# GpSimd's residual row scalings of the second layer: from the retention core into the rotary and gate items

## The chip, the cores and the metric

The kernel runs on one core of a Trainium2 chip, in one launch. The metric is device time in microseconds (us) from the start to the end of that launch. The kernel before took 2866.8 us, the median of three runs (2865.53 to 2873.29).

A core has five engines with queues of their own: TensorE (matmuls, PE in the profile, with its weight loads as PEld), VectorE (DVE), ScalarE (ACT), GpSimd (POOL) and SyncE (SP), which here only issues DMA transfers. ScalarE and GpSimd can issue transfers too. All transfers share 16 DMA engines.

## The reference

The model is a trunk of two layers on one sequence of 1024 rows of 1024 features, in float32. Layer 0 mixes with a gated delta network, layer 1 with retention; each layer ends with a gated feed-forward network. What matters here is the second layer's first half:

```python
for i in range(DEPTH):
    mod = (e @ ada_w[i] + ada_b[i])[:, None, :]
    sh1, sc1, g1, sh2, sc2, g2 = jnp.split(mod, 6, axis=-1)
    y = mixers[i % N_MIXERS](x * (1.0 + sc1) + sh1)
    x = layer_norm(DN_ALPHA * x + (1.0 + g1) * y, ln_g[i, 0], ln_b[i, 0])
    y = conv_ffn(x * (1.0 + sc2) + sh2, ffn_up[i], ffn_conv_w[i], ffn_conv_b[i], ffn_down[i])
    x = layer_norm(DN_ALPHA * x + (1.0 + g2) * y, ln_g[i, 1], ln_b[i, 1])

def retention(h, w_in, w_out):
    q, k, v, gate = jnp.split(h @ w_in, [H * dk, 2 * H * dk, 2 * H * dk + H * dv], axis=-1)
    ...
    q = _chunk_heads(rot(q), H, C)
    k = _chunk_heads(rot(k), H, C) * (dk ** -0.5)
    ...
    o = _standardize(o, 1e-6).reshape(b_, s, H * dv)
    o = o * jax.nn.silu(gate.astype(F32))
    return o.astype(h.dtype) @ w_out
```

The layer norm that ends layer 0 is kept in two parts. The standardized rows go to DRAM (`xs[1]`), and the scaling by `ln_g` and `ln_b` is folded into the projections that read them. The residual `DN_ALPHA * x` of layer 1 needs the scaled rows, `xs[1] * ln_g + ln_b`; they are computed separately and stored in `xg[0]`. That computation is the **residual row scaling**.

## The kernel before

**Tiles and number format.** Every matmul operand is split into a high and a low part (function `split`: ScalarE writes the rounded copy, L89, VectorE the rest, L90), and each product is three matmuls (L110 to L112). A plain tile is 128 partitions by 512 or 1024 floats. Tiles come from rings with a fixed number of buffers for each tag (`BUFS`); the tags that matter are `xT` (2 buffers of 1024 floats), `lane` (4 of 1024), `auh` (8 of 512), `wr` (2 of 1024, raw weights as loaded). A tile is freed when its last reader is done, and the next tile of the tag can be taken then.

**The order of instructions.** The program is traced in Python. A scheduler then orders each engine's queue before the run: it goes by the order of tracing, and takes a later instruction earlier if that one's operands and buffers are free by its own timeline. `after(key)` (L94) ties an instruction behind another one of its queue; the key `"wi"` is the second weight load of the latest seven-product item. Each queue then runs in that order.

**The stages of layer 1.**

1. *Rotary and gate items* (about 1380 to 1702 us in the profile): queries, keys and gates. `strassen(..., direct=True)` (called at L1917) runs 16 items; two of them are done with plain products, the other 14 (n = 2 to 15) in `wino` (L1401), each a 2 by 2 block product with seven block products of 12 matmuls (L1340 and L110 to L112). Each item loads two raw weight tiles of 512 KB (L1405, L1406), VectorE forms the sums of their blocks (`psub`, L1394), and `block` splits them. `rope_item`'s sink (L1884) turns the queries and keys by the tables of angles (`trig`, loaded at L1873 in `auh` tiles), `gate_item`'s sink (L1906) applies the gate's function; both store through ScalarE's queue.
2. *Retention core* (about 1702 to 2070 us): `core(h)` (L1975) goes through eight chunks for each of four heads, while `ret_v` (L1928) computes the values for coming heads in the gaps. TensorE's order is pinned here. For every chunk `ret_back` (L2020) takes statistics of the output on VectorE, one power on GpSimd (L2026), the normalization on VectorE (L2030), a transpose on TensorE, the gate's product (L2051), and for chunks 4 to 7 four sums on GpSimd (L2062). In chunks 0 to 3 of each head, and in chunk 4 of the last, it also calls one `gain_step` (L2027).
3. *Output projection* of the retention with the residual: it reads `xg[0]` with `load_row` (L309). Its modulation row `(1, 2)` comes from `bg_ada` (L234), whose eight 512 KB weight tiles (`mvw`, L240) are `xT` tiles here and whose sums run on VectorE (L250, L252).

**The scalings before.** `gain_step(m)` (L2097) does three things: it scales the block that was loaded by the step before (two GpSimd instructions of 128 by 512, L2100 and L2101) and stores it through SyncE (L2102); every eighth time it takes two `auh` tiles and loads `ln_g` and `ln_b`, spread over the partitions (L2108); and it loads the next block of 128 rows by 512 columns of `xs[1]` into a `lane` tile (L2111). There are 16 blocks: two column halves of eight row blocks.

**A second path for the same work.** The feed-forward items of both layers use `bg_gain` (L406). It puts 16 units into the list `rowq`; `row_step` (L134) scales the block that was loaded by the unit before (L424, L425), stores it through GpSimd's queue (L426) and starts the next unit's load (L418, an `xT` tile, tied behind `"wi"`). The last unit of a column half is scaled at once. `wino` calls `row_step` at its end from the sixth item on (`n > 4`, L1439). The vectors are in two `auh` tiles (L414). While the rotary and gate items run before the change, `rowq` is empty.

Of the kernel before, what the change touches and what calls it, by code (L numbers as in the profile page):

```python
# [15 lines left out]
P = 128  # L16
# [17 lines left out]
def trunk_kernel(ctx: ExitStack, tc, A):  # L34
# [11 lines left out]
    def tl(tag, shape, dt=F32, name=None):  # L46
        return sb.tile(shape, dt, tag=tag, name=name or tag, bufs=BUFS[tag])

    def two(tag, dt=F32, name=None):
        if tag in ("qkv", "auh"):  # L50
            return tl(tag, [P, HALF], dt, name), tl(tag, [P, HALF], dt, name)
        t = tl(tag, [P, 2, HALF], dt, name)
        return t[:, 0], t[:, 1]
# [28 lines left out]
    def hs(half):  # L82
        return slice(half * HALF, (half + 1) * HALF)
# [35 lines left out]
    def bg_step(tile=mm_tile):  # L119
        bg_ps[0] = tile  # L120
        for p in pend:
            p[0] -= 1
        while pend and (pend[0][0] <= 0 or not bg):
            pend.pop(0)[1]()
            if not bg:
                break
        if bg:
            nxt = bg.pop(0)()
            if nxt:
                pend.append(list(nxt))  # L130
# [3 lines left out]
    def row_step():  # L134
        if rowp:
            rowp.pop()()
        if rowq:
            nxt = rowq.pop(0)()
            if nxt:
                rowp.append(nxt[1])  # L140
# [262 lines left out]

    xg = [dr.tile([S, D], F32, tag=f"xg{i}", name=f"xg{i}") for i in range(3)]

    def bg_gain(n, src, dst, tag="lane"):  # L406
        gb = []

        def unit(c, r):
            if r == 0:  # L410
                gb[:] = [tl("auh", [P, HALF], name="gb") for _ in range(2)]
                with after("wi") if tag == "xT" else nullcontext():
                    for t, nm in zip(gb, ("ln_g", "ln_b")):
                        sp.dma_start(t, A[nm][n:n + 1, hs(c)].to_broadcast([P, HALF]))  # L414
            x = tl(tag, [P, HALF], name="xg")
            rs = slice(r * P, r * P + P)
            with after("wi") if tag == "xT" else nullcontext():
                sp.dma_start(x, src[rs, hs(c)])  # L418
            if r == 7:
                return gain(x, rs, c)  # L420
            return 1, lambda: gain(x, rs, c)

        def gain(x, rs, c):
            pool.tensor_tensor(x, x, gb[0], ALU.mult)  # L424
            pool.tensor_tensor(x, x, gb[1], ALU.add)  # L425
            (sp if tag == "lane" else pool).dma_start(dst[rs, hs(c)], x)  # L426

        for c in range(2):
            for r in range(8):
                (bg if tag == "lane" else rowq).append(lambda c=c, r=r: unit(c, r))  # L430
# [903 lines left out]
    def strassen(hT0, xts, scale, shift, items, tags=("hTb", "hTb", "qkv", "qkv", "aux"), direct=False, late=()):  # L1334
# [62 lines left out]
        def drain(n):  # L1397
            for _ in range(min(n, len(late))):
                late.pop(0)()

        def wino(n, sink):  # L1401
            ua, ub = items[n][:2]
            early = bool(late)
            wa, wb = tl("wr", [P, D]), tl("wr", [P, D])
            sp.dma_start(wa, ua)  # L1405
            anchor["wi"] = sp.dma_start(wb, ub)  # L1406
            a11, a12, a21, a22 = wa[:, hs(0)], wa[:, hs(1)], wb[:, hs(0)], wb[:, hs(1)]
            def copy_of(X, tag="cv"):
                t = tl(tag, [P, 516] if tag == "cv" else [P, HALF], name="pc")[:, 0:HALF]
                act.activation(t, X, AF.Copy)  # L1410
                return t

            X = prod(a11, "11")
            p1 = copy_of(X)
            s1 = psub(a21, a22, ALU.add)
            sink(0, prod(a12, "21"), p1)
            s2 = psub(s1, a11)
            Z = prod(s1, "T1")
            z5 = copy_of(Z)
            w2 = block(s2)  # L1420
            s4 = psub(a12, s2)
            drain(2)
            prod(None, "T2", X, w2)
            u2 = copy_of(X)
            s3 = psub(a11, a21)
            drain(2)
            prod(s4, "22", Z)
            sink(1, Z, u2)
            if not early:
                bg_step()  # L1430
            drain(2)
            prod(s3, "T3", X)
            u3 = copy_of(X, "t2")
            sink(3, X, z5)
            drain(2)
            sink(2, prod(a22, "T4"), u3)
            if not early:
                bg_step()
            if n > 4:  # L1439
                row_step()  # L1440

        bg_tag[0] = "lane"
# [461 lines left out]
    def gate_item(u):  # L1904
        def start():
            def sink(q, a, b):  # L1906
                c = c_of(q, a, b) if b is not None else tl("cv", [P, 516], name="sg")[:, 0:HALF]
                act.activation(c, a if b is None else c, AF.Silu)
                act.dma_start(gd[u + q // 2][:, hs(q % 2)], c)
            return sink  # L1910
        return A["ret_wg"][u], A["ret_wg"][u + 1], start, None
# [2 lines left out]
    ropes = [rope_item(h, j) for h in range(RH) for j in range(2)]  # L1914
    gates_ = [gate_item(u) for u in range(4, 16, 2)]
    mixed = [(ropes if q == "r" else gates_).pop(0) for q in "rrgrgrrgrgrrgg"]
    B = strassen(h0, xts, sc_r, sh_r, [gate_item(0), gate_item(2)] + mixed, ("hTa", "aux", "qkv", "qkv", "hTa"), True)  # L1917
    hT = [h0, []]
    xlo = []
    for t in range(4):  # L1920
# [99 lines left out]
    def ret_back(h, n, po):  # L2020
        st = tl("st", [P, 2, 6], name="rst")
        dve.bn_stats(st[:, 0], po)
        mv = tl("s8", [P, 4], name="mv")
        dve.bn_aggr(mv[:, 0:2], st[:, 0])
        dve.tensor_scalar(mv[:, 2:3], mv[:, 1:2], 1e-6, None, ALU.add)
        pool.tensor_tensor(mv[:, 3:4], mv[:, 2:3], mhalf[:, 0:1], ALU.pow)  # L2026
        if n < 4 or h == RH - 1 and n == 4:  # L2027
            gains.pop(0)()
        on = tl("t2", [P, HALF], name="on")
        anchor["on"] = dve.tensor_scalar(on, po, mv[:, 0:1], mv[:, 3:4], ALU.subtract, ALU.mult)  # L2030
        s4 = slice(n % 4 * P, (n % 4 + 1) * P)

        def pair_view(t):
            return t.rearrange("p (j a f) -> p a j f", a=2, f=P)

        def blk(nm):
            return od[2 * h:2 * h + 2, ABLK.index(nm), :, s4].rearrange("j p t -> p j t")

        if n > 3:
            pv = pair_view(tl("cv", [P, 516], name="op")[:, 0:HALF])  # L2040
            for a, nm in enumerate(("11", "12")):
                sp.dma_start(pv[:, a], blk(nm))
        yield RL["b"]
        sl = slice(n * P, (n + 1) * P)
        g = tl("cv", [P, 516], name="gt")[:, 0:HALF]
        sp.dma_start(v4(g), gd[4 * h:4 * h + 4, :, sl].rearrange("j p t -> p j t"))
        pt = mm_tile()
        for j in range(4):
            ptr(pt[:, j * P:(j + 1) * P], on[:, j * P:(j + 1) * P])
        ot = tl("cv", [P, 516], name="ot")[:, 0:HALF]  # L2050
        dve.tensor_mul(ot, pt, g)  # L2051
        ov = pair_view(ot)
        if n < 4:
            for a, nm in enumerate(("11", "12")):
                anchor["x", 1] = act.dma_start(blk(nm), ov[:, a])
            if n == 3:
                emit(("ob", h), RL["o"])
            return
        act.dma_start(blk("22"), ov[:, 1])
        for d, x, y, op, nm in ((ov[:, 0], ov[:, 0], ov[:, 1], ALU.add, "S1"), (pv[:, 0], ov[:, 0], pv[:, 0], ALU.subtract, "S2"),  # L2060
                                (pv[:, 1], pv[:, 1], pv[:, 0], ALU.subtract, "S4"), (ov[:, 1], ov[:, 1], pv[:, 0], ALU.subtract, "S3")):
            pool.tensor_tensor(d, x, y, op)  # L2062
            (pool if n == NCH - 1 and h == RH - 1 else sp).dma_start(blk(nm), d)
# [28 lines left out]
        assert next(mix[0]) == "ops"  # L2092

    mix = []
    gains, gx = [], []

    def gain_step(m):  # L2097
        if gx:
            x, c, rs, gb = gx.pop()
            pool.tensor_tensor(x, x, gb[0], ALU.mult)  # L2100
            pool.tensor_tensor(x, x, gb[1], ALU.add)  # L2101
            sp.dma_start(xg[0][rs, hs(c)], x)  # L2102
        if m < 2 * NCH:
            c, r = divmod(m, NCH)
            if r == 0:
                gbs.append([tl("auh", [P, HALF], name="gb") for _ in range(2)])
                for t, nm in zip(gbs[-1], ("ln_g", "ln_b")):
                    sp.dma_start(t, A[nm][1:2, hs(c)].to_broadcast([P, HALF]))  # L2108
            rs = slice(r * P, r * P + P)
            x = tl("lane", [P, HALF], name="xg")  # L2110
            sp.dma_start(x, xs[1][rs, hs(c)])  # L2111
            gx.append((x, c, rs, gbs[-1]))

    gbs = []
    gains += [lambda m=m: gain_step(m) for m in range(2 * NCH + 1)]
    events["core", -1] = clk[0]
    free["qkv"] = 20
    bg_tag[0] = "xT"
# [105 lines left out]
```

## Time and profile before

| | us |
|---|---|
| median of three runs | 2866.8 |
| the profiled execution: its time | 2872.47 |
| the profiled execution: its span | 2870.7 |
| TensorE busy (97% of the span) | 2785.2 |
| VectorE busy (76%) | 2183.3 |
| ScalarE busy (45%) | 1294.0 |
| GpSimd busy (17%) | 500.2 |
| mean granted TensorE clock, share of full speed | 0.994 |

The span runs from the first to the last instruction on the core. The profiled execution's own time is 1.8 us longer than that and 5.7 us above the median. A stage is read from the windows view, which gives each engine's busy time in a stretch; what an engine waited for is read from the waits view and, in brackets, from the timeline; a line such as `L2101 POOL TENSOR_TENSOR xg<-xg,gb` is line 2101 of the kernel, its engine, its operation and the tiles it writes and reads. Windows are in us from the start of the span.

### The profile page before, as it was taken

The page shows a single profiled execution, that of the slowest core. Times are in us where ns is not written, and L with a number is a line of the kernel's source. Part 1 is how long each engine was busy: PE and PEld are TensorE (multiplying, and loading weights), DVE is VectorE, ACT ScalarE, POOL GpSimd, SP SyncE. Part 2 cuts the span into 40 slices and gives each one's busy share as a digit, 9 for nine tenths or more (in the row PEclk, how much of TensorE's full clock was granted, in tenths as well). Part 3 has the DMA queues.
Part 4 walks back from the last instruction along what each step waited for, and adds up shares of the span by engine and source line. Part 5 has one row for each costly group of instructions (what it writes and reads, how often), then busy time and mean ns, then how long its engine had stood idle before and what let it go on. Part 6 is the DMA issues. An engine that isn't in the chain of part 4 may idle for free.

```text
span 2870.7 us, 38939 instructions
## 1 busy us (share of the span) xinstructions
PE 2785.2 (97%) x13594; PEld 2277.0 (79%) x13594; DVE 2183.3 (76%) x3874; ACT 1294.0 (45%) x2377; POOL 500.2 (17%) x517
## 2 busy tenths in 40 slices
PE   8999999999999999999999999999999999999997
PEld 6787878877787788887888887777787778888886
DVE  6887678676788888778677656666788887777869
ACT  3763465344644444546433342222344644444443
POOL 0411321000023233100000002333301033332001
PEclk9999999999999999999999999999999999999999
DMA  8323242174254555945343364665854253444853
GB/s 279 101 90 115 92 140 92 61 250 150 99 180 168 192 183 172 336 126 180 128 147 119 121 204 153 200 196 160 275 194 147 74 194 132 143 139 161 320 150 118
DMA packets 254292, 465.31 MB, mean 162 GB/s; under 512 B 24400, under 2 KB 81104, under 8 KB 254096
## 3 DMA queue, kind: packets, MB, share of 16 engines
q1 hardware_dynamic: 219776, 407.50, 43.0%
q10 hardware_dynamic: 31488, 46.15, 4.4%
q0 software_dynamic: 2832, 9.18, 0.8%
q8 instruction: 107, 1.75, 0.2%
q14 instruction: 89, 0.73, 0.1%
HBM read 346.86 MB, written 115.87 MB: 161 GB/s over the span
## 4 chain that ended last, share of the span: by engine, by line
PE 56%; DVE 21%; DMA 11%; ACT 6%; issue 5%; POOL 1%; SPq 0%; ACTq 0%; DVEq 0%; POOLq 0%
PE acc L747 10%; PE acc L1340 5%; PE acc L110 4%; PE sc L747 4%; PE acc L111 4%; PE acc L112 4%; PE sc L1340 3%; PE acc L1636 3%; DMA mvw<-in_ada_w 3%; DVE o L1787 3%; DMA wr<-in_ffn_up 2%; PE mm L747 2%; DVE wb L90 2%; DVE qkv L507 2%; DVE mm L1394 1%
## 5 line engine op out<-in xcount | busy, mean ns | idle before, releaser
L747 PE MATMUL acc<-hT,wh 128*128 128x512 f32 x960 | 299.7, 393 | 0.0
L1636 PE MATMUL acc<-bb,ab 128*128 128x512 f32 x984 | 229.8, 392 | 6.5 <-DVE ab L90 4.1
L89 ACT ACTIVATE ab<-ar 128x512 fp32r<-128x512 f32 x210 | 131.1, 629 | 217.0 <-PE mm L316 55.1
L1636 PEld LDWEIGHTS acc<-bb,ab 128*128 128x128 f32 x984 | 183.0, 188 | 48.6 <-DVE ab L90 4.7
L747 PEld LDWEIGHTS acc<-hT,wh 128*128 128x128 f32 x960 | 182.5, 190 | 35.6
L1340 PE MATMUL acc<-T,wb 128*128 128x512 f32 x840 | 202.0, 389 | 0.4 <-DVE wb L90 0.4
L90 DVE TENSOR_TENSOR ab<-ar,ab 128x512 fp32r<-128x512 f32 x210 | 148.7, 715 | 68.5 <-ACT ab L89 68.1
L747 PE MATMUL acc<-hT,wl 128*128 128x512 f32 x480 | 197.3, 411 | 1.2 <-ACT sq L531 0.7
L89 ACT ACTIVATE wb<-mm 128x512 fp32r<-128x512 f32 x216 | 124.4, 597 | 163.0 <-DVE mm L1394 150.1
L1340 PEld LDWEIGHTS acc<-T,wb 128*128 128x128 f32 x840 | 157.5, 188 | 33.8 <-ACT o L1788 1.1
L90 DVE TENSOR_TENSOR wl<-wr,wh 128x1024 fp32r<-128x1024 f32 x95 | 118.6, 1249 | 74.3 <-ACT wh L89 72.6
L1818 POOL TENSOR_TENSOR o<-o 128x512 f32<-128x512 f32 x80 | 119.0, 1496 | 270.1 <-DVE o L1810 167.9
L90 DVE TENSOR_TENSOR wb<-wr,wb 128x512 fp32r<-128x512 f32 x162 | 114.2, 706 | 65.7 <-ACT wb L89 65.6
L89 ACT ACTIVATE wh<-wr 128x1024 fp32r<-128x1024 f32 x95 | 100.6, 1060 | 138.3 <-PE acc L747 61.4
L1787 DVE SCALAR_TENSOR_TENSOR o<-g,vc,o 128x512 f32<-128x512 f32 (+2 forms) x176 | 152.2, 875 | 8.9 <-ACT o L1782 7.7
L90 DVE TENSOR_TENSOR wb<-mm,wb 128x512 fp32r<-128x512 f32 x216 | 144.5, 682 | 7.4 <-ACT wb L89 7.4
L89 ACT ACTIVATE wb<-wr 128x512 fp32r<-128x512 f32 x162 | 101.2, 626 | 95.5 <-PE acc L1340 28.8
L1394 DVE TENSOR_TENSOR mm<-wr 128x512 f32<-128x512 f32 x108 | 83.9, 777 | 71.4 <-DMA wr<-in_ffn_up 58.2
L747 PE MATMUL acc<-wh,hT 128*128 128x512 f32 x384 | 134.3, 412 | 2.1 <-DVE vv L90 2.1
L1410 ACT ACTIVATE pc<-acc 128x512 f32<-128x512 f32 x143 | 84.4, 591 | 111.8 <-PE acc L1340 63.6
L252 DVE SCALAR_TENSOR_TENSOR ada<-mvw,e,ada 128x512 f32<-128x512 f32 x140 | 105.8, 755 | 24.0 <-DMA mvw<-in_ada_w 23.8
L110 PE MATMUL acc<-T,wb 128*128 128x512 f32 x292 | 114.9, 394 | 3.6 <-DVE wb L90 3.3
(677 smaller groups left out, 7356.2 us busy)
## 6 DMA issues: line engine op xcount, KB each, us to landing
wr<-in_ffn_up SPq DMA_DIRECT2D x92, 512.0 KB, 3.9
mvw<-in_ada_w SPq DMA_DIRECT2D x80, 512.0 KB, 4.3
ad<-o SPq DMA_DIRECT2D x154, 256.0 KB, 2.3
ar<-ad SPq DMA_DIRECT2D x154, 256.0 KB, 4.2
Br<-in_ffn_down SPq DMA_DIRECT2D x88, 256.0 KB, 5.2
wr<-in_ret_wv SPq DMA_DIRECT2D x32, 512.0 KB, 3.6
ar<-od SPq DMA_DIRECT2D x56, 256.0 KB, 4.5
wr<-in_gdn_wqkv SPq DMA_DIRECT2D x24, 512.0 KB, 3.9
```

The source lines that it names most:

```text
L89: anchor["sp"] = act.activation(dst_h, src, AF.Copy)
L90: eng.tensor_tensor(dst_l, src, dst_h, ALU.subtract)
L110: mm(acc, wl[:, k], hl[0], start=first, stop=False)
L111: mm(acc, wh[:, k], hl[1], start=False, stop=False)
L112: mm(acc, wh[:, k], hl[0], start=False, stop=last)
L252: dve.scalar_tensor_tensor(a, wr[:, kk], e[:, k:k + 1], a, ALU.mult, ALU.add)
L747: pq(pe.matmul(out, lhsT, rhs, start=start, stop=stop), cost or COST[out.shape[-1]])
L1340: return pe.matmul(*a, skip_group_check=True, **kw)
L1394: dve.tensor_tensor(t, x, y, op)
L1636: return pe.matmul(*args, skip_group_check=True, **kw)
L1787: dve.scalar_tensor_tensor(tv, gv[:, c0 - j:c1 - j], w[:, 2 - j:3 - j], tv, ALU.mult, ALU.add)
L1818: (dve if fp == 0 else pool).tensor_tensor(o[d], o[x], o[y], op)
```

## The change

The calls of `gain_step` in the core go, with the function. Ahead of the rotary and gate items `bg_gain` is called for `xs[1]` and `xg[0]`, with a new switch `own=True` that puts both vectors into one `xT` tile instead of two `auh` tiles; the row blocks use the other `xT` tile. In the direct form of `strassen`, `row_step` is called at the end of every seven-product item and once more inside every item whose number divides by three. What would be left over is done behind the items.

```diff
-    def bg_gain(n, src, dst, tag="lane"):
+    def bg_gain(n, src, dst, tag="lane", own=False):
         gb = []
 
         def unit(c, r):
             if r == 0:
-                gb[:] = [tl("auh", [P, HALF], name="gb") for _ in range(2)]
+                gb[:] = two("xT", F32, "gb") if own else [tl("auh", [P, HALF], name="gb") for _ in range(2)]
                 with after("wi") if tag == "xT" else nullcontext():
...
             sink(1, Z, u2)
             if not early:
                 bg_step()
+            if direct and n % 3 == 0:
+                row_step()
             drain(2)
             prod(s3, "T3", X)
...
                 bg_step()
-            if n > 4:
+            if n > 4 or direct:
                 row_step()
...
+    bg_gain(1, xs[1], xg[0], "xT", True)
     B = strassen(h0, xts, sc_r, sh_r, [gate_item(0), gate_item(2)] + mixed, ("hTa", "aux", "qkv", "qkv", "hTa"), True)
+    while rowq or rowp:
+        row_step()
...
         pool.tensor_tensor(mv[:, 3:4], mv[:, 2:3], mhalf[:, 0:1], ALU.pow)
-        if n < 4 or h == RH - 1 and n == 4:
-            gains.pop(0)()
         on = tl("t2", [P, HALF], name="on")
...
-    gains, gx = [], []
-
-    def gain_step(m):
-        if gx:
-            x, c, rs, gb = gx.pop()
-            pool.tensor_tensor(x, x, gb[0], ALU.mult)
-            pool.tensor_tensor(x, x, gb[1], ALU.add)
-            sp.dma_start(xg[0][rs, hs(c)], x)
-        if m < 2 * NCH:
-            c, r = divmod(m, NCH)
-            if r == 0:
-                gbs.append([tl("auh", [P, HALF], name="gb") for _ in range(2)])
-                for t, nm in zip(gbs[-1], ("ln_g", "ln_b")):
-                    sp.dma_start(t, A[nm][1:2, hs(c)].to_broadcast([P, HALF]))
-            rs = slice(r * P, r * P + P)
-            x = tl("lane", [P, HALF], name="xg")
-            sp.dma_start(x, xs[1][rs, hs(c)])
-            gx.append((x, c, rs, gbs[-1]))
-
-    gbs = []
-    gains += [lambda m=m: gain_step(m) for m in range(2 * NCH + 1)]
```

## The prediction

> **What bounds the kernel now.** I first read the busy time of each engine by stage, because the change takes work out of one stage (the retention core, 1736 to 2024 us) and puts it into an earlier one (the rotary and gate items, 1437 to 1702 us), and because two other stages already do the same kind of work: the feed-forward items of layer 0 (816 to 1130 us) and of layer 1 (2310 to 2610 us) each hold 16 row scalings on GpSimd.
>
> ```profile
> core 0: us, PE busy (x) PEld busy (x) DVE busy (x) ACT busy (x) POOL busy (x), PEclk, DMA share, GB/s
> 816.00:1130.00 314.00, 308.49 (x1354) 251.73 (x1354) 265.72 (x409) 146.33 (x293) 100.97 (x79) 0.99 0.54 184
> 1437.00:1702.00 265.00, 263.37 (x1158) 216.82 (x1157) 194.68 (x311) 98.72 (x174) 0.00 (x0) 1.00 0.44 144
> ...
> 1736.00:2024.00 288.00, 283.66 (x1279) 218.79 (x1277) 186.75 (x344) 69.75 (x118) 99.93 (x108) 0.99 0.61 188
> 2024.00:2070.00 46.00, 43.40 (x191) 32.24 (x190) 33.31 (x59) 14.51 (x28) 15.92 (x21) 1.00 0.77 241
> 2310.00:2610.00 300.00, 297.36 (x1304) 244.12 (x1303) 233.95 (x342) 136.57 (x232) 95.19 (x76) 1.00 0.43 144
> ```
>
> TensorE is the bound on both sides of the move. In the items it is idle for 265 - 263.37 = 1.63 us, in the core for 288 - 283.66 = 4.34 us. GpSimd is quite empty in the items (0.00) and busy for a third of the core. So the first thing to see is a ceiling: whatever leaves the core can give back little more than 4.34 us. Next I read what TensorE waited for, first in the core, then in the items.
>
> ```profile
> PE sc L747 <- DVE on L2030: 2.8, 3, 2.0
> PE acc L747 <- DVE vv L90: 1.1, 3, 0.7
> PE mm L750 <- DVE on L2030: 0.4, 2, 0.2
> ...
> PE acc L1340 <- ACT pc L1410: 1.6, 3, 0.8
> ```
>
> In the core nearly half of the idle time is one wait of 2.0 us. I followed it back, with the timeline of DVE, that of SyncE, the chain that ended last, and narrow windows:
>
> ```profile
> 1929.67 0.37 SPq L2111 DMA_DIRECT2D xg<-xs  x1
> ...
> 1930.98 0.38 SPq L240 DMA_DIRECT2D mvw<-in_ada_w  x1
> ...
> 1930.98 5.92 DMA mvw<-in_ada_w
> ...
> 1936.99 1.19 DVE L252 SCALAR_TENSOR_TENSOR ada<-mvw,e,ada 128x512 f32<-128x512 f32 x1 [1.80 <-DMA mvw<-in_ada_w]
> ...
> 1930.00:1935.00 5.00, 5.00 (x26) 3.61 (x25) 4.86 (x10) 0.78 (x2) 0.03 (x1) 1.00 1.00 293
> ...
> 1940.00:1945.00 5.00, 4.44 (x18) 3.98 (x19) 4.92 (x8) 0.48 (x1) 0.00 (x0) 0.66 0.46 158
> ```
>
> A 512 KB tile of modulation weights (mvw) took 5.92 us with the DMA engines full (share 1.00), DVE stood 1.80 us in front of it, the chunk's statistics and then TensorE stood behind DVE. After the gap the granted clock was 0.66 for 5 us, a loss of 0.34 x 5 = 1.7 us. So the place costs 2.0 + 1.7 = 3.7 us, and 1.3 us ahead of the slow load the same queue had issued a 256 KB load of a row block (xg), which the change removes from here.
>
> **The change part by part.** *What leaves the core.* These are GpSimd's groups there, and the transfers:
>
> ```profile
> L2101 POOL TENSOR_TENSOR xg<-xg,gb 128x512 f32<-128x512 f32 x16 | 22.6, 1413 | 1.3
> L2100 POOL TENSOR_TENSOR xg<-xg,gb 128x512 f32<-128x512 f32 x16 | 22.6, 1411 | 415.3 <-DMA xg<-xs 410.9 <-issue 4.4
> L2026 POOL TENSOR_TENSOR mv<-mv,mhalf 128x1 f32<-128x1 f32 x28 | 17.9, 639 | 57.9 <-DVE mv L2025 49.5 <-DMA od<-ot 8.5
> ...
> xg<-xs SPq DMA_DIRECT2D x16, 256.0 KB, 2.7
> xg<-xg SPq DMA_DIRECT2D x16, 256.0 KB, 2.7
> ...
> SPq L2102 <- POOL xg L2101: 40.9, 15, 6.2
> SPq L2111 <- DMA xg<-xg: 24.4, 10, 3.8
> ```
>
> GpSimd loses 22.6 + 22.6 = 45.2 us, SyncE's queue 32 transfers of 256 KB (and four for the two vectors), and 40.9 + 24.4 = 65.3 us in which that queue stood still with value-weight loads behind it. What would that give TensorE? The power that each chunk needs (L2026, in front of the normalization L2030) never waited for a scaling: its idle time ends with DVE or with a store of the gated output, neither of which moves. No wait of TensorE in the core is put down to a weight load. So 45.2 us of GpSimd and 65.3 us of queue lie beside TensorE's matmuls and are worth nothing by themselves. What is left is the slow mvw load. Without the row load it is issued 0.4 us earlier (the row's 0.37), and 262 KB less are ahead of it, at 293 GB/s 0.89 us: 1.3 us earlier in all. DVE's wait of 1.80 us becomes 0.5 us, TensorE's 2.0 us becomes 0.7 us; a third of the wait, so I leave a third of the clock's loss, 0.6 us. Gain 3.7 - 1.3 = **2.4 us**. Its bounds: 0 (the load is then late for another reason, Bw loads of the output projection stand in the same queue) and 4.34 + 1.7 = 6.0 us (all idle time of the stage and the clock's loss).
>
> The Trainium skill, page "TensorE: Matmul & The Clock Gate", part 1, says that the clock falls to half only after an idle window of about 3.4 us. By it the gap of 2.0 us would cost 2.0 us and the gain would be 1.3 us. The row with 0.66 after a 2 us gap speaks against it, so the trace's price stands.
>
> The freed tiles (two auh, one lane) let loads of a later head start sooner; as no TensorE wait in the core ends with such a load, I count nothing, and the ceiling above holds it.
>
> *What comes into the items.* The same 32 instructions, 16 loads on SyncE, four vector loads, and 16 stores that now go out from GpSimd. A step is done at the end of each seven-product item and once more inside every third: 19 chances for 16 row blocks, so they are through by the twelfth of fourteen items. An item is 84 matmuls of 263.37 / 1158 = 0.227 us, 19.1 us. A row block's tile is held from load to store; prices from the feed-forward stage, where GpSimd does issue the stores:
>
> ```profile
> L426 POOL DMA_DIRECT2D xg<-xg x32: 580/582/759, 827.9 to 2607.9; - x32
> ...
> xg<-xs SPq DMA_DIRECT2D x16, 256.0 KB, 4.6
> xg<-xg POOLq DMA_DIRECT2D x16, 256.0 KB, 2.5
> ```
>
> 4.6 + 1.41 + 1.41 + 0.58 + 2.5 = 10.5 us, and 16 x 10.5 = 168 us fit into 12 x 19.1 = 229 us. GpSimd has nothing else there. The DMA traffic grows by 36 x 0.262 = 9.4 MB over 229 us, 41 GB/s, to 185 GB/s, which is the 184 of the layer-0 feed-forward row.
>
> The **new wait** is that one of the two xT tiles now holds the two vectors, so each row load waits for the store of the block before. Behind that load in SyncE's queue stand the next item's two weight loads, and DVE, ScalarE and then TensorE wait for those. How late may they be? One item, from four timelines:
>
> ```profile
> 1484.75 0.33 SPq L1406 DMA_DIRECT2D wr<-in_ret_wqk  x1
> ...
> 1490.57 0.70 DVE L1394 TENSOR_TENSOR mm<-wr 128x512 f32<-128x512 f32 x1 [2.66 <-DMA wr<-in_ret_wqk]
> ...
> 1492.73 0.69 DVE L90 TENSOR_TENSOR wb<-mm,wb 128x512 fp32r<-128x512 f32 x1 [0.73 <-ACT wb L89]
> ...
> 1497.40 0.23 PE acc L110
> ```
>
> DVE already waits for the second weight tile, yet its block is ready at 1493.42 us and TensorE takes it up at 1497.40 us: a cover of 4.0 us per item. A row load that only shares the DMA engines (0.9 to 1.8 us for 262 KB at 293 or 144 GB/s) is hidden by it.
>
> GpSimd and DVE also slow each other where both run. In the core:
>
> ```profile
> 1740.45 1.80 DVE L90 TENSOR_TENSOR wl<-wr,wh 128x1024 fp32r<-128x1024 f32 x1 [1.35 <-ACT wh L89]
> 1741.25 2.15 POOL L2101 TENSOR_TENSOR xg<-xg,gb 128x512 f32<-128x512 f32 x1
> ...
> 1748.80 1.22 DVE L90 TENSOR_TENSOR wl<-wr,wh 128x1024 fp32r<-128x1024 f32 x1
> ```
>
> 0.58 us more for DVE beside a scaling; 16 times that is 9 us, against 265 - 194.68 = 70 us in which DVE is idle in the items.
>
> For the sum of both effects I take the stages that already hold 16 scalings. Their idle time of TensorE is 314 - 308.49 = 5.51 us and 300 - 297.36 = 2.64 us; at the items' rate (1.63 in 265) those stretches would have 1.93 and 1.85 us. So 16 scalings, and the gate sums that those stages also put on GpSimd, cost at most 3.6 and 0.8 us. The items have DVE 73% busy, the two stages 85% and 78%: nearer to the second. I take **1.5 us**, bounds 0 and 3.6.
>
> **Sum**: -2.4 + 1.5 = -0.9 us. The profiled execution took 2872.47 us (span 2870.7), so 2871.6 against it; it lies 5.7 us above the median of the runs shown, 2866.8, inside their spread. Against the median: **2865.9 us**. A measurement of this kernel can tell about 0.3% from no change, 8.6 us here. This is no change.
>
> **The rivals.**
>
> *All idle time goes* (2858 us). The core's 6.0 us and the 2.60 us of the stretch behind it (46 - 43.40) vanish and the items stay as they are: 8.6 us. For it: the queue is freer by 65 us. Against it: most of those waits end with DVE and with stores that stay.
>
> *The row load blocks the weights* (2895 us, slower). The order of SyncE's queue is fixed before the run. If a row load is put right behind the step that scales the block before, the queue stands from the start of that scaling to its store's landing, 1.41 + 1.41 + 0.58 + 2.5 = 5.9 us, 1.9 us more than the cover. Fifteen reloads: 29 us. It decides from 4.0 us of standing on. For it: the core's row, where SyncE stood 2.7 us on average for a scaling that was late. Against it: in the items SyncE waits for room anyway, and 10.5 us fit into 19.1.
>
> *The modulation weights lose their tiles* (2878 us, slower). They use xT too:
>
> ```profile
> L240 SPq DMA_DIRECT2D mvw<-in_ada_w x8: 368/378/410, 1409.4 to 1934.1; - x8
> ...
> 1445.48 9.05 SPq L240 DMA_DIRECT2D mvw<-in_ada_w  x3
> ```
>
> Six of the eight tiles are loaded by about 1454 us, before or early in the items, and the last two only at 1930.98 and 1934.09, the stall above. With row blocks and vectors in xT the early loads may come later, inside the full core. Three more stalls of 3.7 us: 11.1 us.
>
> *The change doesn't do what it says* (2867 us): an mvw tile holds the second xT tile through the items until the core frees it, and row blocks slip back into the core; then the time is as before, since 45.2 us of GpSimd are hidden there too.
>
> *DVE is locked out* (2889 us). If each of the 32 scalings stopped a DVE instruction for half of its 1.41 us, 22.6 us, all of it on TensorE's path: 2866.8 + 22.6. Against it: the 70 us and the cover. The Trainium skill, page "SBUF — State Buffer", section "Who interferes with whom", speaks for it: a DVE instruction with two SBUF inputs and a GpSimd one that reads SBUF exclude each other, the second waits to the end of the first. The two lengthened rows agree.
>
> **How the numbers follow.** Chances: forecast 0.70 (its own range 2860 to 2873, from -6.0 to +3.6 us around the median and the runs' spread); all idle time goes 0.05; doesn't do what it says 0.06; modulation weights 0.10; blocked weights 0.06; locked out 0.03. The range of 2859 to 2879 us holds the first, third and fourth of these and leaves 0.14 out. Faster by over 0.3%: 0.05; within: 0.70 + 0.06 = 0.76; slower: 0.10 + 0.06 + 0.03 = 0.19.
>
> **What would show it.** GpSimd is busy for some 45 us between about 1445 and 1680 us, and has no full-width scalings behind 1736. TensorE's idle time in the core falls below 4 us, the clock at the second mvw load stays near 1. In the items it stays under 5 us. I am wrong if TensorE waits there for blocks whose weight loads SyncE issued late, if the mvw loads move into the core with new DVE waits, or if scalings still run behind 1736 us.

## The result and the profile after

The changed kernel takes 2881.49 us (median of 5 runs), the kernel before 2867.5 us on the same chip: ratio 1.0054, 95% interval 1.0041 to 1.0067 (taken over all runs, so not exactly that of the medians). It is 14 us slower, where 2865.9 us and no change were forecast. The profiled execution took 2880.61 us (span 2878.8).

The windows view of the changed kernel, same columns as before (the stages lie some 13 us later behind the items):

```profile
1437.00:1702.00 265.00, 254.33 (x1103) 207.22 (x1102) 201.02 (x310) 95.85 (x169) 52.25 (x45) 0.99 0.50 167
1736.00:2024.00 288.00, 282.49 (x1279) 218.17 (x1278) 182.28 (x334) 69.36 (x116) 53.85 (x74) 1.00 0.51 153
2310.00:2610.00 300.00, 299.82 (x1317) 246.40 (x1316) 234.70 (x346) 139.55 (x237) 97.38 (x77) 1.00 0.45 150
```

GpSimd's work has moved (52.25 us in the items, 53.85 instead of 99.93 in the core), so the change does what it says. TensorE's idle time in the items went from 1.63 to 10.67 us, and VectorE is busy for 6.3 us more although the change gave it no new work.

Fixed windows cut the stages at other places once they have shifted. So I measure stages between two instructions that all kernels share, from the tile views of `bt` and `kz` (count, shortest/median/longest ns, first and last start). First the kernel before, then the changed one:

```profile
L454 ACT ACTIVATE bt<-mm,fh,fs x8: 772/773/782, 1392.6 to 1409.8; 128x512 f32<-128x512 f32 x8
...
L1966 ACT ACTIVATE kz<-mm,vc x28: 474/476/477, 1737.2 to 2035.1; 128x256 fp32r<-128x256 f32 x28
```

```profile
L454 ACT ACTIVATE bt<-mm,fh,fs x8: 772/774/782, 1393.5 to 1410.8; 128x512 f32<-128x512 f32 x8
...
L1971 ACT ACTIVATE kz<-mm,vc x28: 473/474/477, 1750.5 to 2046.5; 128x256 fp32r<-128x256 f32 x28
```

**Items** are from the first `bt` to the first `kz`: 344.6 us before, 357.0 after (+12.4). **Core** is from the first to the last `kz`: 297.9 before, 296.0 after (-1.9). Together +10.5 us. The spans of the two profiled executions differ by 8.1 us: these 10.5, 0.9 more ahead of the items and 3.3 less behind the core. What is ahead and behind is taken as scatter between single executions: the stretch behind the core has the same instructions in all kernels below and lasted 831.2 to 835.6 us. The medians differ by 14.

What TensorE waited for in the items, from the waits view of the changed kernel (total, times, longest, in us):

```profile
PE sc L110 <- DVE wb L90: 3.1, 1, 3.1
PE acc L1340 <- ACT pc L1410: 2.1, 2, 1.7
PE acc L1340 <- DVE wb L90: 1.7, 2, 0.9
PE sc L1340 <- ACT pc L1410: 1.6, 2, 1.4
PE acc L110 <- DVE wb L90: 1.6, 1, 1.6
PE sc L1340 <- DVE wb L90: 0.4, 1, 0.4
```

All of these end with VectorE's split (`wb`) or ScalarE's copy (`pc`). Two patterns lie behind them. The first, on the timeline of the changed kernel (start, duration, engine, line):

```profile
1518.52 1.28 POOL L424 TENSOR_TENSOR xg<-xg,gb 128x512 f32<-128x512 f32 x1 [4.58 <-DMA xg<-xs]
1519.05 1.30 DVE L1897 TENSOR_TENSOR pc<-pc,trig 128x512 f32<-128x512 f32 x1
...
1519.88 1.62 POOL L425 TENSOR_TENSOR xg<-xg,gb 128x512 f32<-128x512 f32 x1
1520.28 1.77 DVE L1898 TENSOR_TENSOR pc<-pc,rm 128x512 f32<-128x512 f32 x1
...
1523.88 0.63 ACT L1910 ACTIVATE pc<-pc 128x512 f32<-128x512 f32 x1 [0.72 <-DVE pc L1324]
1524.38 0.68 DVE L1899 TENSOR_TENSOR pc<-pc,rm 128x512 f32<-128x512 f32 x1
...
1525.80 0.94 PE L1340 MATMUL acc<-22_12748,wb 128*128 128x512 f32 x3 [0.90 <-DVE wb L90]
```

A block's two scalings fell into a burst: a stretch in which VectorE runs rotary instructions, sums and splits back to back. Two rotary instructions took 1.30 and 1.77 us where their neighbours take 0.68. The burst ended 1.71 us late, and the split behind it let TensorE stand for 0.90 us.

The second pattern concerns the modulation weights `mvw` of row (1, 2). The line view of the changed kernel and its timeline:

```profile
L240 SPq DMA_DIRECT2D mvw<-in_ada_w x8: 368/378/383, 1650.9 to 1947.4; - x8
```

```profile
1645.33 0.33 SPq L418 DMA_DIRECT2D xg<-xs  x1
1647.86 1.62 POOL L424 TENSOR_TENSOR xg<-xg,gb 128x512 f32<-128x512 f32 x1 [4.85 <-DMA xg<-xs]
1649.55 1.29 POOL L425 TENSOR_TENSOR xg<-xg,gb 128x512 f32<-128x512 f32 x1
1650.87 7.18 SPq L240 DMA_DIRECT2D mvw<-in_ada_w  x3
...
1655.31 0.49 DVE L250 TENSOR_SCALAR ada<-mvw,e 128x512 f32<-128x512 f32 x1 [6.98 <-DMA mvw<-in_ada_w]
...
1658.31 0.64 PE L110 MATMUL sc<-T,wb 128*128 128x512 f32 x1 [3.11 <-DVE wb L90]
```

Before, the first load started at 1409.4 us. Now none starts until the last scaling has read the vectors, which frees that `xT` tile at 1650.85 us. The sums that read the weights moved with them, the first from 1439 to 1655 us, and stand in VectorE's queue ahead of an item's splits. So VectorE stood 6.98 us and TensorE 3.11 us.

### The profile page after: what moved, and what is told of

The parts are those of the page before. It is cut to its first block, busy times and chain, and to the rows that moved or that the text cites. A ratio compares the mean times of both kernels' runs of the same rounds, so it can differ in the third digit from the quotient of the medians.

```text
span 2878.8 us, 38937 instructions
## 1 busy us (share of the span) xinstructions
PE 2788.2 (97%) x13594; PEld 2278.3 (79%) x13594; DVE 2190.1 (76%) x3874; ACT 1294.0 (45%) x2377; POOL 508.7 (18%) x533
## 4 chain that ended last, share of the span: by engine, by line
PE 57%; DVE 20%; DMA 12%; ACT 5%; issue 4%; POOL 1%; SPq 0%; ACTq 0%; DVEq 0%; POOLq 0%
PE acc L747 10%; PE acc L1340 5%; PE sc L747 4%; PE acc L110 4%; PE acc L111 4%; PE acc L112 4%; PE acc L1638 3%; PE sc L1340 3%; DMA mvw<-in_ada_w 2%; PE mm L747 2%; DVE o L1789 2%; DMA wr<-in_ffn_up 2%; DVE wb L90 2%; DVE qkv L507 2%; DVE mm L1394 1%
## 5 line engine op out<-in xcount | busy, mean ns | idle before, releaser
L1340 PE MATMUL acc<-T,wb 128*128 128x512 f32 x840 | 202.1, 389 | 0.5 <-DVE wb L90 0.4
L424 POOL TENSOR_TENSOR xg<-xg,gb 128x512 f32<-128x512 f32 x48 | 68.2, 1422 | 596.5 <-DMA xg<-xs 596.5
```

The costliest lines, as they stand in the source:

```text
L1340: return pe.matmul(*a, skip_group_check=True, **kw)
```

## The experiments

Three explanations were to be told apart: the **weights** (late `mvw` tiles), the **queue** (row loads ahead of tables and weights in SyncE's queue, and their traffic) and the **lock-out** (GpSimd's scalings stop VectorE's instructions). The stages are measured as above, in the one profiled execution of each run; the ratios are to the kernel before on the same chip.

| run | items | core | median us | before | ratio, 95% interval |
|---|---|---|---|---|---|
| before | 344.6 | 297.9 | | | |
| changed | 357.0 | 296.0 | 2881.49 | 2867.5 | 1.0054 (1.0041 to 1.0067) |
| e1_mv_core | 351.5 | 299.6 | 2878.65 | 2866.35 | 1.0043 (1.0025 to 1.006) |
| e2_no_inner | 350.0 | 295.3 | 2874.79 | 2866.35 | 1.0031 (1.0018 to 1.0044) |
| e3_x_own | 361.8 | 294.9 | 2883.55 | 2866.35 | 1.006 (1.0045 to 1.0075) |
| e6_own_noinner | 356.2 | 295.7 | 2881.36 | 2866.35 | 1.0053 (1.0038 to 1.0068) |
| e7_writes_only | 344.5 | 299.3 | 2872.51 | 2869.5 | 1.0012 (1.0001 to 1.0023) |
| e8_loads_only | 344.3 | 299.2 | 2871.24 | 2869.5 | 1.001 (1.0 to 1.002) |
| e10_gate_steps | 351.4 | 297.0 | 2877.68 | 2869.5 | 1.0024 (1.0011 to 1.0037) |
| e11_copy | 344.4 | 295.4 | 2868.64 | 2869.5 | 1.0 (0.9991 to 1.001) |
| e12_copies | 346.0 | 300.2 | 2871.77 | 2868.91 | 1.0005 (0.9996 to 1.0014) |
| e13_changed_with_fills | 347.2 | 297.5 | 2871.68 | 2868.91 | 1.0011 (1.0 to 1.0022) |
| e5_before_weights_in_core | 345.4 | 299.1 | 2871.88 | 2868.91 | 1.001 (1.0001 to 1.0019) |
| e14_late_and_spread | 357.6 | 295.2 | 2878.29 | 2868.91 | 1.0035 (1.0022 to 1.0049) |

### Where the weights are loaded: e1, e2, e3, e6

e1 ties the `mvw` loads behind the latest value weight, so that they lie in the core:

```diff
-            sp.dma_start(wr, A["ada_w"][i, ...])
+            with after("w" if (i, j) == (1, 2) else None):
+                sp.dma_start(wr, A["ada_w"][i, ...])
```

> The changed kernel with one edit: the eight loads of the modulation weights of the row (1, 2) are tied behind the latest value-weight load, so that none of them and none of their VectorE sums lies in the rotary and gate items. Theory A (the modulation weights lost their tiles: their first load lands at 1655 us, VectorE stands 7.0 us before it in the items, TensorE 3.1 + 1.4 + 1.7 us with 1.7 us of clock behind it): TensorE's idle time in the items falls from 10.7 us to under 5 us, and the core costs up to one stall of 3.7 us more: 2874 to 2878 us. Theory B (SyncE's queue stands before row loads and the weight loads come late): idle time in the items stays near 10 us, 2881 us or more.

The stalls near 1660 us are gone and the items are 5.5 us shorter than in the changed kernel, but still 6.9 us longer than before; the core is longer by 3.6. So the weights are one cause of the longer items, and there is another. The time, 2878.65 us, lies between the two expectations, and the intervals of e1 and of the changed kernel overlap: the whole times don't tell these two apart, the stages and the stalls do.

e2 takes the additional steps inside every third item away:

```diff
-            if direct and n % 3 == 0:
-                row_step()
```

> The changed kernel without the additional step inside every third seven-product item: 14 chances for 16 row blocks, the last two done behind the items. The order of SyncE's queue then has no pair of row loads in front of the tables of angles, and the modulation weights move into the core. Theory A: like the kernel with the tied loads, 2874 to 2878 us. Theory B: the TensorE waits at about 1467, 1526 and 1584 us, 0.8 + 0.9 + 0.5 us, which follow such pairs, are gone too; with A and B together 2872 to 2875 us. If neither holds, 2881 us.

The time lies in the range of the weights alone and in that of weights and queue together, so it doesn't choose between them. The order of the queue put the weights behind the items proper, at 1711 us and later, and the stall went with them. On e2's timeline:

```profile
1719.29 0.49 DVE L250 TENSOR_SCALAR ada<-mvw,e 128x512 f32<-128x512 f32 x1 [11.01 <-DMA mvw<-in_ada_w]
...
1721.75 0.50 PE L747 MATMUL acc<-wl,hT 128*128 128x512 f32 x1 [3.26 <-DVE wl L90]
```

Ahead of this, TensorE has one new stall in the items, of 1.78 us at 1443, while the `T` tiles are built. Behind it comes a stretch in which neither e1 nor e2 sums modulation weights. The windows view of e1 and then of e2:

```profile
1446.00:1705.00 259.00, 254.73 (x1113) 209.08 (x1112) 193.66 (x295) 95.30 (x169) 51.97 (x45) 0.99 0.49 163
1446.00:1705.00 259.00, 258.90 (x1141) 213.68 (x1140) 191.77 (x297) 96.56 (x170) 46.70 (x42) 1.00 0.50 167
```

e2 scales 14 blocks here and e1 15. TensorE is idle for 4.27 us in e1, whose additional steps lie inside items, and for 0.10 us in e2, whose steps lie at their ends. Both lengthen VectorE's instructions (in e2 one rotary line, `rm<-pc,trig` at L1893, takes 1024 ns on average and the other five 679 to 686). So where in an item a scaling falls decides whether TensorE pays for it. The end of an item is not always free either: e6, whose steps are there too, has a stall of 1.25 us at 1486 us, ahead of its first weight load, and e14 one of 2.08 us at 1676.

e3 gives the row blocks a tile of their own, so that an `xT` tile is left for the weights; e6 does that without the inner steps:

```diff
-            x = tl(tag, [P, HALF], name="xg")
+            x = tl("xr" if own else tag, [P, HALF], name="xg")
```

> The changed kernel with the row blocks in one tile of their own (512 floats, one buffer), so that xT's second tile is left to the modulation weights; the row load still waits for the store of the block before. Theory A: the modulation weights are loaded one after the other through the items, no VectorE wait of 7 us, idle time of TensorE in the items under 5 us, 2873 to 2877 us. Theory B: the waits for weight blocks remain or grow, since one more transfer per item stands in SyncE's queue: 2880 us or more.

> Both edits: row blocks in a tile of their own and no additional step inside every third item. Theory A and B together: the items near the 1.6 us of idle time that they had before, and the core's gain kept: 2866 to 2870 us. If the cost is that GpSimd and VectorE slow each other (theory C), it stays at 2876 us or more in all four kernels.

e3's 2883.55 us lies in the range given to the queue, which e7 and e8 clear below, and e6's 2881.36 in that of the lock-out; both are above what the weights alone would have left. With a tile of their own the weights come one by one in the middle of the items. In e6 VectorE waits 8.0 us for them there, and a stall of 1.7 us follows. In e3 it waits only 1.1 us for them; TensorE's longest stall, 4.5 us, has another history, as e3's timeline shows:

```profile
1578.12 2.77 DVE L252 SCALAR_TENSOR_TENSOR ada<-mvw,e,ada 128x512 f32<-128x512 f32 x2
...
1587.40 1.59 DVE L1897 TENSOR_TENSOR pc<-pc,trig 128x512 f32<-128x512 f32 x1
1588.92 1.75 DVE L1898 TENSOR_TENSOR pc<-pc,rm 128x512 f32<-128x512 f32 x1
...
1593.12 0.80 PE L110 MATMUL sc<-T,wb 128*128 128x512 f32 x1 [4.54 <-DVE wb L90]
```

VectorE runs without a gap from 1576 to 1595 us here: the modulation sums have come into a full stretch, and sums (0.74 us each elsewhere) and rotary instructions are lengthened beside scalings. A free tile alone is no cure.

### What of the scaling costs time: e7, e8, e12, e13

These start from e1 (e13: from the changed kernel), keep every load and store, and replace only what GpSimd does to a block: six fills in e7 and e13, nothing in e8, four copies in e12.

```diff
-            pool.tensor_tensor(x, x, gb[0], ALU.mult)
-            pool.tensor_tensor(x, x, gb[1], ALU.add)
+            pool.memset(x, 0.0)
...
+            pool.tensor_copy(x, gb[0])
```

> Base: e1 (modulation weights tied into the core; items 6.9 us longer than before, TensorE stalls of 2.07 us at 1444, 0.52 at 1471, 1.56 at 1492, 0.78 at 1531). Here GpSimd's two scalings of each of the 16 blocks are replaced by six fills of the same block (measured in this kernel at 0.53 us each, 3.2 us together instead of 2.9): GpSimd stays as busy and the load-scale-store chain as long, but its instructions read no SBUF. xg[0] then holds zeros, so the residual of layer 1 is left out. Theory lock-out (a GpSimd instruction that reads SBUF and a VectorE one with two SBUF inputs exclude each other): the four stalls above go, the rotary item's VectorE instructions fall back from 0.85 to 0.89 us to about 0.68, the items last 344 to 347 us, and the time is 2869 to 2873. Theory queue and DMA (the row loads stand ahead of tables and weights): the stalls stay, the items last 350 to 353 us, 2877 to 2880.

> As e1, but GpSimd only passes the blocks through: the row loads and the stores stay, the 32 scalings are left out, so xg[0] holds unscaled rows. Lock-out: as with the fills, items 344 to 347 us, 2869 to 2873. Queue and DMA: items 349 us or more, 2876 or more. If this run is short and the fills' run is not, it is the length of the chain (the time that a block's tile stays taken) and not the port.

The items last 344.5 and 344.3 us, as before the change. In both, the instructions of TensorE, VectorE and SyncE run in the same order as in e1, and ScalarE's up to a few swaps. So every row load keeps its place, and the queue is cleared. e7 keeps GpSimd as busy (53.22 us in the items' window) and the chain of load, work and store as long, and its instructions write and do not read: all of the 6.9 us by which e1's items were too long go. That is the lock-out, and here the whole times agree: the intervals of e1 and e7 do not overlap.

> As the run with the fills, but the scalings of each block are replaced by four GpSimd copies of a gain tile into the block: one SBUF input instead of none (fills) or two (scalings); xg[0] then holds the gains, so the residual of layer 1 is left out. If reading SBUF at all is what excludes VectorE's instructions with two SBUF inputs: items 349 to 353 us as in e1 (351.5), rotary VectorE instructions lengthened, 2875 to 2879. If only GpSimd instructions with two SBUF inputs do it: items 344 to 346 us as with the fills, 2870 to 2874.

346.0 and 2871.77 us: by the numbers this is the expectation that only GpSimd instructions with two SBUF inputs exclude. The trace speaks against it, since the rotary instructions at `rm` do lengthen, to 722 and 786 ns on average. And GpSimd waits too. Two of its pairs of copies on e12's timeline:

```profile
1506.20 1.30 POOL L425 COPY xg<-gb 128x512 f32<-128x512 f32 x2 [12.22 <-DMA xg<-xs]
...
1518.50 4.14 POOL L425 COPY xg<-gb 128x512 f32<-128x512 f32 x2 [8.12 <-DMA xg<-xs]
```

During the second pair VectorE's burst runs on at 0.68 us an instruction. So one SBUF input on GpSimd's side is enough for the two engines to hold each other up. Why it costs the items less is argued and not shown: a copy takes 0.65 us when nothing holds it, so VectorE can lose less behind one than behind a scaling of 1.3 to 1.6 us. e12 is also not as clean as e7, since three row loads and a weight load stand at other places of SyncE's queue than in e1, and some VectorE instructions too.

> The changed kernel itself (modulation weights not tied), with six fills in place of each block's two scalings; xg[0] holds zeros. Tests whether the two causes add. If they do, the lock-out's 7.0 us go and the 5.5 us of the modulation weights in the items stay: TensorE's stalls of 3.1, 1.4 and 1.7 us near 1660 remain, items 349 to 351 us, core 296, 2870 to 2876. If the weights' stalls come only because the lock-out makes the items late: items 344 to 346 us, 2865 to 2869.

347.2 us, between both expectations: without the lock-out the late weights cost 2.6 us in the items, with it 5.5 (changed kernel against e1). The two costs are not simply added. In e13 the first weight load starts 244.8 us after the first `bt` and VectorE does not wait for it, in the changed kernel 257.4 us after. VectorE's order differs there too (SyncE's does not), so how one cause feeds the other is not isolated. By rows of the line view, VectorE's groups in the items, first of the changed kernel, then of e13 (total us, mean ns):

```profile
L1895 DVE TENSOR_TENSOR rm<-pc,trig 128x512 f32<-128x512 f32 x16 | 14.2, 888 | 0.0
L1898 DVE TENSOR_TENSOR pc<-pc,rm 128x512 f32<-128x512 f32 x16 | 13.5, 846 | 0.0
...
L90 DVE TENSOR_TENSOR T<-bt,T 128x512 fp32r<-128x512 f32 x16 | 12.1, 791 | 6.5 <-ACT T L89 6.5
L1897 DVE TENSOR_TENSOR pc<-pc,trig 128x512 f32<-128x512 f32 x16 | 12.0, 751 | 0.0
L1899 DVE TENSOR_TENSOR pc<-pc,rm 128x512 f32<-128x512 f32 x16 | 11.4, 711 | 0.0
```

```profile
L1895 DVE TENSOR_TENSOR rm<-pc,trig 128x512 f32<-128x512 f32 x16 | 10.9, 683 | 0.0
...
L1899 DVE TENSOR_TENSOR pc<-pc,rm 128x512 f32<-128x512 f32 x16 | 10.9, 680 | 0.0
L1898 DVE TENSOR_TENSOR pc<-pc,rm 128x512 f32<-128x512 f32 x16 | 10.9, 679 | 0.0
L90 DVE TENSOR_TENSOR T<-bt,T 128x512 fp32r<-128x512 f32 x16 | 10.4, 685 | 6.7 <-ACT T L89 6.7
```

All five have two inputs in SBUF. They sum to 63.2 us in the changed kernel and, with 10.9 for L1897 too, to 54.0 in e13: 9.2 us more of VectorE. The items differ by 9.8 us. That the two are so close is no rule. From the first `bt` to the first `kz`, VectorE is busy for 245.72 us in e1 and 234.51 in e7, 11.2 us more, and the items are 7.0 us longer. It is busy for 247.53 us in e2 and 239.06 before, 8.5 us more, and most of e2's rotary and gate items run without a wait of TensorE (0.10 us, above).

The Trainium skill, page "SBUF — State Buffer", section "Who interferes with whom", says that a VectorE instruction with two SBUF inputs contends with a GpSimd instruction that reads SBUF and not with one that only writes it. The runs agree on both halves: 888 ns beside scalings, 683 beside fills.

### What the move could have brought: e11, e5

e11 leaves the scalings out and copies `xs[1]` to `xg[0]` in one transfer behind the items.

> The scalings are left out altogether: behind the items one transfer copies xs[1] to xg[0] (4 MB, unscaled rows). This is the most that taking them out of the core can give. All theories: the items as before (344 to 346 us), the core 2 us shorter than before (296), 2862 to 2866. If it is 2860 or less, the core holds a larger cost of the scalings than the 1.9 us that the changed kernel gained there.

The stages are as expected, the time is not: 2868.64 against 2869.5 us, ratio 1.0. Even without any scaling nothing is gained that can be measured.

e5 is the kernel before with e1's tie.

> The kernel before, its scalings still in the core, with one line changed: the eight modulation weight loads tied into the core, as in e1. The run with the fills has a core of 299.3 us and the run with the copy, whose weights are early, 295.4: so 3.9 us for late weights. If they cost the same here, the core is 300 to 302 us instead of 297.9, the items 344 to 345, and the time 2869 to 2874. The prediction's rival of the modulation weights said three more stalls of 3.7 us, 11.1 us, 2878 or more.

Cores have to be compared at the same granted clock, because it falls in some of them behind the stall at the late modulation load and not in others. The windows view from the first to the last `kz`, for the kernel before, the changed one, e11 and e13, and then the slice of e13 with the fall (the slice of the kernel before is the one with 0.66 in the prediction):

```profile
1737.20:2035.10 297.90, 293.44 (x1323) 226.16 (x1323) 195.41 (x361) 72.86 (x125) 100.48 (x109) 0.99 0.61 188
1750.50:2046.50 296.00, 291.46 (x1322) 224.77 (x1322) 193.27 (x361) 72.67 (x124) 55.99 (x77) 1.00 0.52 158
1741.00:2036.40 295.40, 291.46 (x1323) 224.88 (x1323) 192.84 (x361) 72.75 (x125) 53.03 (x77) 1.00 0.52 158
1732.00:2029.50 297.50, 293.05 (x1323) 226.18 (x1322) 192.39 (x361) 72.72 (x124) 53.44 (x77) 0.99 0.52 157
...
1935.00:1940.00 5.00, 5.00 (x20) 4.37 (x21) 4.22 (x8) 0.78 (x2) 0.00 (x0) 0.66 0.55 172
```

The kernel before and e13 have the fall, and last 297.9 and 297.5 us with TensorE idle for 4.46 and 4.45 us, although only the first has scalings there. The changed kernel and e11 have none, and last 296.0 and 295.4 us. So most of the 2.5 us by which e11's core is shorter than before is the clock and not the scalings. With late weights and no fall, e5 (with scalings) lasts 299.1 us and e8 (without) 299.2. Under equal conditions the scalings cost nothing in the core. e5's core is only 1.2 us longer than before, below the expected 2 to 4, but the kernel before has a fall in it and e5 has none: TensorE is idle for 6.51 us in e5's core.

### Other places: e10, e14

```diff
-            if direct and n % 3 == 0:
+            if direct and n in (4, 6, 9, 11, 14, 15):
...
-            if n > 4 or direct:
+            if n > (3 if direct else 4):
```

> As e1, but the steps begin two items later (first row load in the fifth item instead of the third, behind the building of the T tiles) and the additional steps inside an item lie in the six gate items and not in every third item, four of which are rotary ones. Lock-out: the stall of 2.07 us at 1444 goes and those of the rotary items shrink; items 347 to 349 us, 2871 to 2875. Queue and DMA: as many row loads in as few items, so no less than e1: 2877 to 2881.

A miss, at a time that had been given to the queue, which e7 and e8 clear. The stall at 1444 us did go (`T<-bt,T` is back at 688 ns), but other bursts were hit, as e10's line view shows:

```profile
L1896 DVE TENSOR_TENSOR rm<-pc,trig 128x512 f32<-128x512 f32 x16 | 15.3, 959 | 0.0
```

Rotary and gate items overlap: on the changed kernel's timeline above, ScalarE's gate function at 1523.88 us lies between rotary instructions. So a step in a gate item still meets them.

e14 drops the inner steps, starts at the fourth item, and calls `row_step` in the core's chunks 0 to 3 for what is left.

> A version that should undo the harm: one step at the end of each item from the fourth item on (behind the building of the T tiles, none inside an item), and what is left over in the first chunks of the core. Lock-out: the stall of 1.8 us at 1443 goes, the items last 346 to 348 us (e2: 350.0), the core 295 to 297 us, 2867 to 2872, no difference from before that can be measured. The run with the copy says that no place of the scalings can gain more than 2.5 us.

A miss, with items of 357.6 us. Its timeline at the start of the core:

```profile
1724.64 0.48 DVE L250 TENSOR_SCALAR ada<-mvw,e 128x512 f32<-128x512 f32 x1 [7.15 <-DMA mvw<-in_ada_w]
...
1735.30 0.80 PE L747 MATMUL acc<-wh,hT 128*128 128x512 f32 x1 [7.87 <-DVE vv L90]
```

The leftover blocks kept the weights out until the core began, VectorE stood 7.15 us for them, and TensorE 7.87 us for the value splits queued behind. No kernel here beats the one before, and by e11 no place of the scalings could by more than a measurement can show.

## Why the prediction was wrong

**The core, -2.4 us.** Measured -1.9, near by luck and for another reason than given. I expected the wait before the chunk to shrink by 1.3 us, from 2.0 to 0.7, as the load got faster. The waits view of the changed kernel's core shows it as before, and the timeline where it is:

```profile
PE sc L747 <- DVE on L2033: 2.8, 2, 2.0
```

```profile
1947.41 0.37 SPq L240 DMA_DIRECT2D mvw<-in_ada_w  x1
...
1949.78 0.75 DVE L252 SCALAR_TENSOR_TENSOR ada<-mvw,e,ada 128x512 f32<-128x512 f32 x1 [1.20 <-DMA mvw<-in_ada_w]
...
1953.93 0.96 PE L747 MATMUL sc<-vv,kz 128*128 128x512 f32 x3 [2.04 <-DVE on L2033]
```

The slice of 5 us behind it, from the windows view:

```profile
1955.00:1960.00 5.00, 5.00 (x24) 3.59 (x24) 4.17 (x10) 0.78 (x2) 0.00 (x0) 1.00 0.75 228
```

VectorE waits less for this load (1.20 instead of 1.80 us), TensorE as long. What went (windows view above, clock third from the end) is the fall of the granted clock behind it, 0.66 before and 1.00 now, which I had priced at 1.7 us. TensorE's idle time in the core, which should have fallen below 4 us, went from 4.46 to 4.54. As e13's core has the fall without any scaling in it, it doesn't take scalings to have the fall, and the 1.9 us are not shown to be a gain of the change at all.

**The items, +1.5 us, bounds 0 and 3.6.** This is the step that failed: measured +12.4 us. The lengthening of VectorE came out near, 9 us (9.2 measured between the changed kernel and e13), though from one instruction of the core and for 16 blocks of two scalings. Then I set it against the 70 us "in which DVE is idle in the items" and took 1.5 us from the idle time of the feed-forward stages. An average does not say where the loss falls. Much of the 70 us are waits between bursts; the scalings of the additional steps fell into the bursts, where VectorE has no gap and TensorE's next weights stand behind it. In e2, with the steps at the items' ends alone, the same kind of loss was nearly free. The feed-forward stages do not run the rotary bursts; that this is why they showed less was not tested. The cover of 4.0 us, read from one item, did hold for the row loads (e7, e8), not for these.

**The rivals.** The *modulation weights* were one of the two causes, with a chance of 0.10: they did lose their tiles, but the stalls came in the items (3.1 and, behind ScalarE's copies, 1.4 and 1.7 us) and not in the core. They are worth 2.6 us alone and 5.5 with the lock-out. The *lock-out* got 0.03 at 22.6 us and was worth 7.0 (e1 against e7) to 9.8 us (changed kernel against e13). Both came true together, a case that the forecast did not hold, and the measured time lies 2.5 us above the range. The *blocked weights* did not happen: e7 and e8 keep every row load in its place in that queue, and their items are as short as before. That *all idle time goes* and that *the change doesn't do what it says* are refuted by the windows above.

**Left open.** Why the late weights cost more beside the lock-out than alone was not taken apart. What makes the clock fall behind one gap of 2 us and not behind another stays open too. Steps at the items' ends alone with the weights tied into the core, e2 and e1 in one, were not tried, nor e14 with its weights tied; by e2's windows such a kernel could come near the one before, by the stalls of e6 and e14 it could stay a few us above.

## What to carry to other kernels

Free time of an engine is no place by itself: ask which instructions run beside the moved work. A GpSimd instruction that reads SBUF can cost TensorE time if it meets a back-to-back burst of VectorE instructions with two SBUF inputs on the path to TensorE, whatever VectorE's average; with its steps at the items' ends alone, e2 paid next to nothing over most of the items (0.10 us of idle time against 4.27 in e1). Before moving work for the sake of a stage, leave it out once (e11): here that showed that there was nothing to gain that could be measured. Before crediting a stage with a gain, compare its granted clock. And when a tile ring gets a new tenant, look up who else loads into it, and what its reader's queue holds behind the wait.

## What was not expected of the hardware

Gaps of 2.0 us in the same chunk left the granted clock at 0.66 in the kernel before and at 1.00 in the changed one; the gap's length alone did not decide it. And the exclusion works both ways: a pair of GpSimd copies that took 1.30 us at the shortest took up to 4.14 us beside a rotary burst (e12), while scalings there lengthened VectorE's instruction from 0.68 to 1.77 us (changed kernel).
